# Fewer projections in step with the first modulation, and gates in two branches, in a two-layer diffusion block on one Trainium2 core

## The chip, the core and the metric

The kernel runs on one core of a Trainium2 chip. Time is the device time of one execution in microseconds (us); smaller is better. A profile is one further execution recorded by the hardware profiler. The engines are TensorE (PE, with its weight loads PEld), VectorE (DVE), ScalarE (ACT), GpSimd (POOL) and SyncE (SP), whose queue issues nearly all transfers.

## The reference, cut to what matters

Two layers work on 256 context and 256 latent tokens with width 2048, in float32. Each layer normalises, applies a shift and a scale that come from a conditioning vector (the modulation), runs a mixer, projects and adds. Layer 0 is a bidirectional gated DeltaNet:

```python
qkv, z, ba = jnp.split(h @ w_in, [DN_CONV_CH, DN_CONV_CH + DN_VW], axis=-1)
q, k, v = jnp.split(short_conv_silu(qkv, conv_w), [DN_QK, 2 * DN_QK], axis=-1)
beta = jax.nn.sigmoid(ba[:, :, :, 0])
g = -jnp.exp(a_log) * jax.nn.softplus(ba[:, :, :, 1] + dt_bias)
...
gc = jnp.cumsum(chunks(g), axis=-1)
decay = jnp.where(incl, jnp.exp(jnp.where(incl, diff, 0.0)), 0.0)
lower = jnp.where(strict, jnp.einsum('nbhid,nbhjd->nbhij', kb, kc) * decay, 0.0)
tinv = triangular_solve(eye + lower, eye)
```

There are 16 key heads ("groups" in the kernel), each with two value heads and two directions, and chunks of tokens that are solved with an inverse and then joined by a recurrence. Layer 1 is differential attention; the change doesn't touch it.

## The kernel before, in words

Tokens lie along the free axis (512 of them), the width along partitions in 16 k-tiles. A float32 projection is done as three matmuls on split operands (hi x hi, hi x lo, lo x hi), 16 k-tiles x 3 matmuls of 512 columns each.

The program has these stages. First the early stage, lines 260 to 325. The modulation of layer 0 is computed by `ada_pair`, 16 pairs of 256 outputs, each from four tiles `ar` of 512 KB (`ada_load`, 12 buffers); each pair ends in a copy (`arow`), small matmuls and `ada_put`. Pair 0 stands ahead of the loads of x (`xt`), which feed the sum of squares (`acc0`) and the row of reciprocal roots (`rrow0`, line 284). Then eight steps follow; each computes two pairs, makes two k-tiles of h (`make_h`: multiply by `rrow0` on GpSimd, scale and shift on ScalarE, split into `hhi` and `hlo`) and runs these two k-tiles of the six projections in the list `EARLY`: ba (the inputs of beta and decay), k0, q0, v00, v01 and k1, in PSUM tiles so, pj, pj, iv, iv and sb. The activated conditioning row `rc` is written to DRAM as `sc_d` from ScalarE's queue (line 324); the later modulations read it back through tiles `cr`.

Then `gates` (lines 375 to 461) turns ba into the tables `gct`, `lnb`, `eg`, `egl`, `kd`: a copy, four transposes, a softplus on both halves at once (line 415 to 427: 512 columns), the product with `ea` (line 434), cumulative sums by matmul, and the same sums as rows through four staging copies `gt_gr` to DRAM as `gc_d` (line 447). `adt` and `convw` are loaded just before, on SP's queue.

After it, generators write the instructions in an order that a planner (`Drive`) sets by priorities and estimated costs. `filler` writes the projections in a fixed order (k0, q0, v0, v1 of group 0, k1, then for each group z0, z1, next q, v0, v1, and k two ahead); those in `early` are only finished. `post_k`, `post_q`, `post_v`, `post_z` do convolution and activation. `stream_m` builds the masked matrices m of a group: `decay` loads rows of `gc_d` into `grm`, subtracts `gct`, takes the exponential; `block_inv` sends them through DRAM (`mb_d`), inverts 16 x 16 blocks on VectorE and stores them in `tu_d`. `stream_lev` joins the blocks in three levels to `uf`. `stream_at` does the same decays (`gra`) for the attention part. `stream_b` runs the recurrence, four steps a group, and needs v, uf and, in each half, at. Two streams compute the other modulations on GpSimd and ScalarE (`aw`, `rp`). A scheduler then fixes the order on each engine from the order written, priorities and a timing model; `tc.high_priority()` puts what it holds ahead.

Last come the two halves of the output projection (from about 2012 us) and layer 1.

Of the kernel before, what the change touches and what calls it, by code (L numbers as in the profile page):

```python
# [20 lines left out]
P = 128  # L21
T = 512
# [39 lines left out]
def body(ctx, tc, D, d, out):  # L62
# [197 lines left out]
    t0_cm = pool("t0")  # L260
# [10 lines left out]
    with tc.high_priority():  # L271
        ada_pair(0, 0, ada_load(0, 0, t0, "ar", 12), gq(), t0)
        xt = [hpool.tile([P, T], F32, tag="hlo", name=f"xt{kt}", bufs=KT) for kt in range(KT)]
        for kt in range(KT):
            nc.sync.dma_start(xt[kt], d["xT"][:, kt])
    with tc.high_priority():
        acc0 = t0.tile([P, T], F32, name="acc0")
        nc.scalar.activation(acc0, xt[0], AF.Square)
        for kt in range(1, KT):
            sq = t0.tile([P, T], F32, tag="mh", name=f"sq{kt}", bufs=2)  # L280
            nc.scalar.activation(sq, xt[kt], AF.Square)
            nc.vector.tensor_tensor(acc0, acc0, sq, ALU.add)
        rrow0 = t0.tile([P, T], F32, name="rrow0")
        nc.scalar.copy(rrow0, rstd_rows(acc0, T, lambda: so().rearrange("p a b i -> p (a b i)"),
                                         t0.tile([P, 4, P], F32, name="rr_dg0")))

    SK = 2
# [7 lines left out]
    np_ = 0  # L295
    for k0 in range(0, KT, SK):
        with tc.high_priority():
            for kind in range(2):
                if k0 + kind:
                    pr = kind * HKT + k0 // 2  # L300
                    ada_pair(0, pr, ada_load(0, pr, t0, "ar", 12), (gq, tr)[np_ % 2](), t0)
                np_ += 1
            for kt in range(k0, k0 + 2):
                make_h((xt[kt][:, 0:256], xt[kt][:, 256:512]), kt, rrow0, 0, hhi, hl, t0, nc.gpsimd)
        for n, src, _ in EARLY:
            w = SK * P
            r = t0.tile([P, w], F32, tag="er", name=f"e{n}r{k0}", bufs=4)
            nc.sync.dma_start(r, src[:, k0 * P:k0 * P + w])
            hi = t0.tile([P, w], F32R, tag="eh", name=f"e{n}h{k0}", bufs=8)
            lo = t0.tile([P, w], F32R, tag="el", name=f"e{n}l{k0}", bufs=8)  # L310
            split(hi, lo, r)
            for k in range(SK):
                kt, ks = k0 + k, slice(k * P, (k + 1) * P)
                ps = early[n]
                mm(ps, hi[:, ks], hhi[:, kt, :], kt == 0, False)
                mm(ps, hi[:, ks], hl(kt), False, False)
                mm(ps, lo[:, ks], hhi[:, kt, :], False, kt == KT - 1)
    rc = t0.tile([2, D], F32, name="rc")
    nc.sync.dma_start(rc, d["crow"])
    rth = t0.tile([2, D], F32, name="rth")  # L320
    nc.scalar.activation(rth, rc, AF.Tanh, scale=0.5)
    nc.vector.scalar_tensor_tensor(rc, rth, 1.0, rc, ALU.add, ALU.mult)
    nc.vector.tensor_scalar(rc, rc, 0.5, None, ALU.mult)
    nc.scalar.dma_start(sc_d, rc)
# [35 lines left out]
    for i in range(2):  # L360
        for j in range(2):
            nc.sync.dma_start(full(tu_d[i][j]), zt.rearrange("p (u i) -> p u i", u=8))
# [128 lines left out]
    def ev(*k):  # L491
        return evs.setdefault(k, Event())
# [802 lines left out]
```

## Time and profile before

| | |
|---|---|
| median of 3 runs | 3181.67 us (3176.39 to 3182.67) |
| the profiled execution | 3170.24 us, its span 3168.5 us |
| busy share of the span | PE 89%, PEld 71%, DVE 62%, ACT 59%, POOL 64% |
| moved by DMA | 457.06 MB, mean 144 GB/s |
| mean granted clock of TensorE | 0.954 of 2.4 GHz |

A share is a mean over stages with different limits, so the stretches of the next section but one count for more than this table. A granted clock of 0.50 is 1.2 GHz.

### The profile page before, as it was taken

The page shows a single profiled execution, that of the slowest core. Times are in us where ns is not written, and L with a number is a line of the kernel's source. Part 1 is how long each engine was busy: PE and PEld are TensorE (multiplying, and loading weights), DVE is VectorE, ACT ScalarE, POOL GpSimd, SP SyncE. Part 2 cuts the span into 40 slices and gives each one's busy share as a digit, 9 for nine tenths or more (in the row PEclk, how much of TensorE's full clock was granted, in tenths as well). Part 3 has the DMA queues.
Part 4 walks back from the last instruction along what each step waited for, and adds up shares of the span by engine and source line. Part 5 has one row for each costly group of instructions (what it writes and reads, how often), then busy time and mean ns, then how long its engine had stood idle before and what let it go on. Part 6 is the DMA issues. An engine that isn't in the chain of part 4 may idle for free.

```text
span 3168.5 us, 52448 instructions
## 1 busy us (share of the span) xinstructions
PE 2833.0 (89%) x16178; PEld 2236.6 (71%) x16178; DVE 1980.1 (62%) x4274; ACT 1863.0 (59%) x5466; POOL 2026.2 (64%) x2370
## 2 busy tenths in 40 slices
PE   4977888888998988998988988899898999999998
PEld 1555666676776766776766766677686888888888
DVE  2148768778778688588688688632334664545454
ACT  3545666666766766766666666654455665434354
POOL 2567677777787777777777777566466677322234
PEclk6988999999999999999999999999999999999999
DMA  9645445455545555545455546656744454333345
GB/s 362 223 114 118 123 119 135 123 133 118 139 134 129 127 126 133 128 129 136 122 125 131 132 118 134 173 171 189 230 147 132 144 164 150 123 110 113 117 127 164
DMA packets 511795, 457.06 MB, mean 144 GB/s; under 512 B 241684, under 2 KB 383764, under 8 KB 511508
## 3 DMA queue, kind: packets, MB, share of 16 engines
q1 hardware_dynamic: 511508, 453.68, 51.8%
q8 instruction: 127, 2.08, 0.3%
q14 instruction: 156, 1.28, 0.1%
q10 hardware_dynamic: 4, 0.02, 0.0%
HBM read 427.18 MB, written 26.36 MB: 143 GB/s over the span
## 4 chain that ended last, share of the span: by engine, by line
PE 33%; DVE 26%; DMA 19%; ACT 7%; POOL 7%; issue 5%; SPq 2%; POOLq 0%; DVEq 0%; ACTq 0%
PE pj L83 28%; DMA gra<-gc_d 5%; POOL rp L138 4%; DMA grm<-gc_d 4%; DVE bP L712 4%; DVE grm L687 3%; DMA aw<-in_adaw_dram 3%; DVE gra L687 2%; DVE bY L714 2%; ACT rp L139 2%; DVE R L783 1%; PE sb L83 1%; DMA ar<-in_adaw_dram 1%; PE iv L83 1%; DVE ma L695 1%
## 5 line engine op out<-in xcount | busy, mean ns | idle before, releaser
L139 ACT ACTIVATE rp<-rp 128x256 f32<-128x256 f32 x1024 | 426.9, 417 | 378.6 <-POOL rp L138 375.5
L712 DVE TENSOR_TENSOR bP<-bX,bY 64x1 f32<-64x1 f32 (+14 forms) x480 | 228.8, 477 | 18.1 <-ACT bY L710 9.8
L139 ACT ACTIVATION_READ_ACCUMULATOR rp<-rp 128x1 f32 x1024 | 194.0, 189 | 0.0
L687 DVE TENSOR_SCALAR gra<-gra,gct,lnb 128x128 f32<-128x128 f32 x256 | 114.3, 488 | 97.9 <-DMA gra<-gc_d 97.2
L687 DVE TENSOR_SCALAR grm<-grm,gct,lnb 128x128 f32<-128x128 f32 x256 | 144.9, 610 | 47.9 <-DMA grm<-gc_d 47.3
L783 DVE TENSOR_TENSOR R<-iv,lv 128x512 f16<-128x512 f32 x192 | 126.1, 678 | 32.8 <-PE iv L83 32.6
L689 ACT ACTIVATE grm<-grm 128x512 f32<-128x512 f32 x64 | 40.4, 631 | 132.0 <-DVE grm L687 127.1
L83 PEld LDWEIGHTS <-m 128*128 128x128 f16 x1024 | 74.2, 100 | 62.0 <-issue 57.7
L714 DVE TENSOR_REDUCE bY<-bP 64x1 f32<-64x1 f32 (+14 forms) x480 | 108.8, 227 | 8.7
L83 PE MATMUL iv<-U,R 128*128 128x128 f16 x768 | 75.7, 223 | 34.4 <-DVE R L783 30.0
L83 PEld LDWEIGHTS <-R 128*128 128x128 f16 x768 | 47.6, 99 | 77.6 <-DVE R L783 44.6
L745 POOL TENSOR_TENSOR ma<-ma,cs 128x512 f32<-128x512 f32 x64 | 85.3, 1333 | 20.7 <-DVE ma L695 18.3
L83 PE MATMUL sb<-yb,uf 128*128 128x128 bf16 x512 | 54.2, 225 | 40.7 <-ACT yb L879 22.2
L689 ACT ACTIVATE gra<-gra 128x512 f32<-128x512 f32 x64 | 40.4, 631 | 84.1 <-DVE gra L687 84.1
L83 PE MATMUL iv<-T,m 128*128 128x128 f16 x768 | 71.4, 223 | 15.8 <-ACT T L800 7.2
L224 DVE TENSOR_TENSOR hlo<-mh,hhi 128x512 fp32r<-128x512 f32 x32 | 29.6, 929 | 86.8 <-ACT hhi L223 77.8
L748 POOL TENSOR_TENSOR ml<-ma,m 128x512 bf16<-128x512 f32 x64 | 76.1, 1189 | 10.5 <-ACT m L747 10.3
L83 PEld LDWEIGHTS <-uf 128*128 128x128 f16 x512 | 36.4, 100 | 64.6 <-issue 59.1
L801 ACT CAST U<-iv 128x512 f16<-128x512 f32 x128 | 75.7, 591 | 0.0
L800 ACT CAST T<-iv 128x512 f16<-128x512 f32 x128 | 73.7, 576 | 3.0 <-PE iv L83 2.9
L83 PE MATMUL so<-x,at 128*128 128x128 f32 x512 | 71.6, 280 | 3.8 <-DVE x L911 2.7
L83 PEld LDWEIGHTS so<-x,at 128*128 128x128 f32 x512 | 64.9, 194 | 6.2 <-DVE x L911 3.6
(2758 smaller groups left out, 11429.3 us busy)
## 6 DMA issues: line engine op xcount, KB each, us to landing
aw<-in_adaw_dram SPq DMA_DIRECT2D x512, 128.0 KB, 3.0
ar<-in_adaw_dram SPq DMA_DIRECT2D x64, 512.0 KB, 7.3
gra<-gc_d SPq DMA_DIRECT2D x128, 128.0 KB, 4.2
grm<-gc_d SPq DMA_DIRECT2D x128, 128.0 KB, 4.1
mb_d<-m SPq DMA_DIRECT2D x32, 256.0 KB, 3.7
T<-tu_d SPq DMA_DIRECT2D x128, 64.0 KB, 2.7
U<-tu_d SPq DMA_DIRECT2D x128, 64.0 KB, 2.7
yd<-sz SPq DMA_DIRECT2D x32, 256.0 KB, 3.4
```

The lines of the kernel that those rows point to most:

```text
L83: nc.tensor.matmul(o, l, r, start=start, stop=stop)
L138: nc.gpsimd.tensor_tensor(pr, r, cr[:, s], ALU.mult)
L139: nc.scalar.activation(pr, pr, AF.Copy, accum_out=acc[:, s, q:q + 1])
L687: nc.vector.tensor_scalar(gr[:, u], gr[:, u], gct[:, c, dd, j:j + 1], lnb[:, c, dd, j:j + 1], ALU.subtract, ALU.min)
L689: nc.scalar.activation(gr, gr, AF.Exp)
L712: nc.vector.tensor_tensor(pr[:, :i, :i], X[:, i, :i].unsqueeze(1).to_broadcast([64, i, i]), Y[:, :i, :i].rearrange("p j c -> p c j"), ALU. ...
L714: nc.vector.tensor_reduce(Y[:, i, :i], pr[:, :i, :i], AX.X, ALU.add)
L745: nc.gpsimd.tensor_tensor(ma, ma, ident.unsqueeze(1).to_broadcast([P, 4, P]), ALU.add)
L748: nc.gpsimd.tensor_tensor(ml[:, :, k], mv, m16[:, :, k], ALU.subtract)
L783: nc.vector.tensor_tensor(R, quad(pp), lvb(n), ALU.mult)
L800: nc.scalar.copy(Tm, quad(pt))
L801: nc.scalar.copy(U, quad(pu))
```

## The change

- x is loaded ahead of everything in the early stage; pair 0 of the modulation goes into the first step.
- `EARLY` keeps only ba, k0 and q0; v00, v01 and k1 become ordinary jobs of `filler`. `iv` now serves the rstd row.
- The tiles of the early stage move to a pool `ta` with 8 `ar` buffers for 12, 6 `er`, `eh` and `el` for 4, 8 and 8; the projections are written inside `tc.high_priority()` too.
- `rc` is laid out over 128 partitions, computed at the very start, and stored to `sc_d` only in `gates`, after the exponential for `eg`.
- `convw` and `adt` are loaded at the end of the early stage, into a pool `gp` that also keeps the tables.
- `gates` takes the two softplus branches apart: decay (256 columns) first, then the row sums in two stores for four, then the beta branch.
- The zeroing of `tu_d` stands behind `gates`.
- `stream_lev` no longer waits for the convolutions of v0 and v1 of group 0; `stream_at` waits for `tu(0, 1)` in group 0.

```diff
+    W2 = 2 * D // P
+    rc = gp.tile([P, W2], F32, name="rc")
+    nc.sync.dma_start(rc, d["crow"].rearrange("s (p i) -> (s p) i", i=W2))
...
-    with tc.high_priority():
-        ada_pair(0, 0, ada_load(0, 0, t0, "ar", 12), gq(), t0)
...
-    EARLY = [("ba", d["wba"], so()), ("k0", d["win"][0, 1], pj()), ("q0", d["win"][0, 0], pj()),
-             ("v00", d["win"][0, 2], iv()), ("v01", d["win"][0, 3], iv())]
-    if G > 1:
-        EARLY.append(("k1", d["win"][1, 1], sb()))
+    EARLY = [("ba", d["wba"], so()), ("k0", d["win"][0, 1], pj()), ("q0", d["win"][0, 0], pj())]
...
+    with tc.high_priority():
+        for kt in range(KT):
+            nc.sync.dma_start(xt[kt], d["xT"][:, kt])
...
+        nc.scalar.copy(rrow0, rstd_rows(acc0, T, iv, ta.tile([P, 4, P], F32, name="rr_dg0")))
+        np_ = 0
+        for k0 in range(0, KT, SK):
             for kind in range(2):
-                if k0 + kind:
-                    pr = kind * HKT + k0 // 2
-                    ada_pair(0, pr, ada_load(0, pr, t0, "ar", 12), (gq, tr)[np_ % 2](), t0)
+                pr = kind * HKT + k0 // 2
+                ada_pair(0, pr, ada_load(0, pr, ta, "ar", 8), (gq, tr)[np_ % 2](), ta)
                 np_ += 1
...
-    nc.scalar.dma_start(sc_d, rc)
...
+        convw = load_small("convw", [P, 4 * KT, 5], d["convw"], gp)
+        adt = load_small("adt", [P, 2, 2, HV],
+                         d["adt"].to_broadcast([P, NB]).rearrange("p (k d h) -> p k d h", k=2, d=2), gp)
...
+        nc.vector.tensor_tensor(t2[1], ba[:, :, :, 1, :], wide(adt[:, 1]), ALU.add)
+        nc.vector.tensor_copy(bt, ba[:, :, :, 0, :])
...
+        def softplus(k):
+            t, e, u, w = t2[k], tl(f"e{k}", sh), tl(f"u{k}", sh), tl(f"w{k}", sh)
+            nc.scalar.activation(e, t, AF.Abs)
+            nc.scalar.activation(e, e, AF.Exp, scale=-1.0)
+            nc.vector.tensor_scalar(u, e, 2.0, None, ALU.add)
+            nc.vector.reciprocal(w, u)
...
+            return w
+
+        w = softplus(1)
+        g = tl("g", sh)
         nc.vector.tensor_tensor(g, w, wide(ea), ALU.mult)
...
+        for a in range(2):
+            p3 = (gq, tr)[a]()
+            for c in range(2):
+                for dd in range(2):
+                    q = 2 * c + dd
+                    mm(p3[:HV, q * P:(q + 1) * P], g[:, 2 * a + c, dd, :], tri(dd))
+            r = tl(f"r{a}", [HV, 4, P])
+            nc.scalar.copy(r.rearrange("p q i -> p (q i)"), p3[:HV])
+            nc.sync.dma_start(gc_d[2 * a:2 * a + 2].rearrange("c (d h) i -> h (c d) i", d=2), r)
...
+        nc.vector.tensor_scalar(lnb, softplus(0), -1.0, None, ALU.mult)
+        tc.keep_in_program_order(nc.scalar.activation(eg, p1v, AF.Exp))
+        tc.keep_in_program_order(nc.scalar.dma_start(sc_d.rearrange("s (p i) -> (s p) i", i=W2), rc))
...
+        nc.vector.tensor_tensor(gct, raw, lnb, ALU.subtract)
...
     def stream_lev(p):
-        yield ev("conv", 0, "v0")
-        yield ev("conv", 0, "v1")
...
             yield ev("kT", g)
             yield ev("qT", g)
+            if g == 0:
+                yield ev("tu", 0, 1)
```

## Rows read from the trace of the kernel before

**Rows 1.** Windows: busy us (x instructions) by engine, clock, DMA share, GB/s.
```profile
0.00:75.00 75.00, 33.35 (x250) 12.20 (x250) 17.41 (x29) 23.03 (x49) 12.53 (x17) 0.65 0.97 363
75.00:186.00 111.00, 105.03 (x628) 65.76 (x628) 14.47 (x18) 59.81 (x174) 73.30 (x100) 0.98 0.62 203
186.00:342.00 156.00, 107.81 (x475) 81.55 (x476) 125.40 (x234) 82.31 (x254) 106.99 (x121) 0.82 0.46 114
342.00:2012.00 1670.00, 1491.56 (x8798) 1151.14 (x8798) 1279.94 (x2957) 1104.59 (x3446) 1246.92 (x1549) 0.96 0.52 129
```

**Rows 2.** Windows, ten microseconds of the early stage, same columns.
```profile
30.00:40.00 10.00, 2.32 (x20) 0.40 (x16) 7.01 (x10) 6.48 (x12) 0.94 (x1) 0.50 1.03 392
```

**Rows 3.** Timeline of ScalarE: start, us, instruction, idle before it and releaser.
```profile
72.00 0.50 ACTq L324 DMA_DIRECT2D sc_d<-rc  x1
72.54 0.59 ACT L284 COPY rrow<-so 128x512 f32<-128x512 f32 x1 [16.20 <-DMA ar<-in_adaw_dram]
```

**Rows 4.** Timeline of TensorE: first and last projection matmuls of the early stage.
```profile
76.70 0.63 PE L83 MATMUL pj<-hhi,ek0h 128*128 128x512 f32 x1
77.13 0.63 PE L83 MATMUL pj<-hhi,eq0h 128*128 128x512 f32 x1
...
184.60 0.40 PE L83 MATMUL sb<-hhi,ek1l 128*128 128x512 f32 x1
184.83 0.60 PE L401 MATMUL gq<-cs,gt_baT 128*128 128x128 f32 x4
```

**Rows 5.** Timeline of ScalarE: first uf; recurrence begins in groups 1 and 15.
```profile
342.20 0.58 ACT L790 CAST uf<-iv 128x512 f16<-128x512 f32 x1
...
441.86 0.61 ACT L879 CAST yb<-v 128x512 bf16<-128x512 f32 x1
...
2030.51 0.61 ACT L879 CAST yb<-v 128x512 bf16<-128x512 f32 x1
```

**Rows 6.** DMA issues from 0 to 186 us: count, KB each, us to landing.
```profile
ar<-in_adaw_dram SPq DMA_DIRECT2D x64, 512.0 KB, 7.3
xt<-in_xT_dram SPq DMA_DIRECT2D x16, 256.0 KB, 6.0
...
ebar<-in_wba_dram SPq DMA_DIRECT2D x8, 128.0 KB, 4.1
```

**Rows 7.** Timeline of TensorE: modulation tiles at full and half clock, small matmuls.
```profile
12.11 0.64 PE L83 MATMUL tr<-ar,sc 128*32 128x256 f32 x8 [0.24 <-DMA ar<-in_adaw_dram]
...
17.89 0.61 PE L83 MATMUL tr<-sel,arow 128*128 128x2 f32 x4
...
62.66 1.08 PE L83 MATMUL gq<-ar,sc 128*32 128x256 f32 x8 [1.68 <-DMA ar<-in_adaw_dram]
```

**Rows 8.** Timeline of VectorE in the gates.
```profile
189.90 0.20 DVE L432 TENSOR_SCALAR gt_ea<-gt_ea 128x64 f32<-128x64 f32 x1 [11.19 <-ACT gt_ea L431]
...
195.76 3.35 DVE L420 RECIPROCAL gt_w<-gt_u 128x512 f32<-128x512 f32 x1
...
212.61 0.94 DVE L434 TENSOR_TENSOR gt_g<-gt_w,gt_ea 128x256 f32<-128x256 f32 x1
...
215.09 1.75 DVE L451 RECIPROCAL beta<-gt_e 128x256 f32<-128x256 f32 x1
...
236.12 1.00 DVE L459 TENSOR_TENSOR gct<-gct,lnb 128x256 f32<-128x256 f32 x1
...
243.38 0.67 DVE L582 COPY kT<-tr 128x512 f32<-128x512 f32 x1
```

**Rows 9.** Timelines of VectorE and SP in the first decays, and the page's DMA issues.
```profile
251.14 1.66 DVE L687 TENSOR_SCALAR gra<-gra,gct,lnb 128x128 f32<-128x128 f32 x4 [1.64 <-DMA gra<-gc_d]
...
267.79 0.38 SPq L701 DMA_DIRECT2D mb_d<-m  x1
...
grm<-gc_d SPq DMA_DIRECT2D x128, 128.0 KB, 4.1
```

**Rows 10.** Weight splits of group 2's k on ScalarE: ns min/median/max, first and last start.
```profile
L185 ACT CAST g2khi<-g2kr x8: 387/410/449, 310.8 to 329.7; 128x256 fp32r<-128x256 f32 x8
```

More of the change, by code (lines that the diff above doesn't have):

```diff
@@ L258, in so @@
         return psm.tile([P, 2, 2, P], F32, tag="so", name="so", bufs=1)
-    t0_cm = pool("t0")
+    gp_cm = pool("gp", side="right")
+    gp = gp_cm.__enter__()
+    gct, eg, kd, egl, lnb = (gp.tile([P, NCH, 2, HV], F32, name=n) for n in ("gct", "eg", "kd", "egl", "lnb"))
+    zt = gp.tile([P, P], F16, name="zt")
+    nc.vector.memset(zt, 0.0)
+    t0_cm = pool("t0", reuse_waits="tile")
     t0 = t0_cm.__enter__()
@@ L305, in body @@
[L305 to L323, printed above, removed]
-    nc.scalar.dma_start(sc_d, rc)
+                make_h((xt[kt][:, 0:256], xt[kt][:, 256:512]), kt, rrow0, 0, hhi, hl, ta, nc.gpsimd)
+            for n, src, _ in EARLY:
+                w = SK * P
+                r = ta.tile([P, w], F32, tag="er", name=f"e{n}r{k0}", bufs=6)
+                nc.sync.dma_start(r, src[:, k0 * P:k0 * P + w])
+                hi = ta.tile([P, w], F32R, tag="eh", name=f"e{n}h{k0}", bufs=6)
+                lo = ta.tile([P, w], F32R, tag="el", name=f"e{n}l{k0}", bufs=6)
+                split(hi, lo, r)
+                for k in range(SK):
+                    kt, ks = k0 + k, slice(k * P, (k + 1) * P)
+                    ps = early[n]
+                    mm(ps, hi[:, ks], hhi[:, kt, :], kt == 0, False)
+                    mm(ps, hi[:, ks], hl(kt), False, False)
+                    mm(ps, lo[:, ks], hhi[:, kt, :], False, kt == KT - 1)
@@ L355, in body @@
     dl = dl_cm.__enter__()
-    zt = dl.tile([P, 1024], F16, name="zt", tag="m16", bufs=4)
-    nc.vector.memset(zt, 0.0)
-    full = lambda a: a.rearrange("u (j i) -> j u i", i=P)[:P]
-    diag = lambda a: bass.AP(tensor=a[:].tensor, offset=a[:].offset, ap=[[16 * P + 16, 64], [P, 16], [1, 16]])
-    for i in range(2):
-        for j in range(2):
-            nc.sync.dma_start(full(tu_d[i][j]), zt.rearrange("p (u i) -> p u i", u=8))
-    convw = load_small("convw", [P, 4 * KT, 5], d["convw"], dl)
@@ L427, in gates @@
-        nc.vector.scalar_tensor_tensor(f5(w2), f5(t2), 0.0, f5(w2), ALU.max, ALU.add)
-        nc.vector.tensor_scalar(lnb, w2[:, 0], -1.0, None, ALU.mult)
-        e, t, w = e2[:, 0], t2[:, 0], w2[:, 1]
-        ea = t1.tile([P, 2, HV], F32, name="ea", tag="jk", bufs=1)
+        t2 = [tl(f"t{k}", sh) for k in range(2)]
+        bt = tl("bt", sh)
+        nc.vector.tensor_tensor(t2[1], ba[:, :, :, 1, :], wide(adt[:, 1]), ALU.add)
+        nc.vector.tensor_copy(bt, ba[:, :, :, 0, :])
+        ea = tl("ea", [P, 2, HV])
@@ L454, in gates @@
-        nc.scalar.activation(egl, p2[:, :n].rearrange("p (c d h) -> p c d h", c=NCH, d=2), AF.Exp)
-        nc.scalar.activation(eg, gct, AF.Exp)
-        nc.vector.tensor_tensor(fl(t), p2[:, :n], fl(gct), ALU.subtract)
+        t = tl("kt", sh)
+        nc.vector.tensor_tensor(fl(t), p1[:, n:2 * n], fl(raw), ALU.subtract)
         nc.scalar.activation(t, t, AF.Exp)
         nc.vector.tensor_tensor(kd, t, beta, ALU.mult)
-        nc.vector.tensor_tensor(gct, gct, lnb, ALU.subtract)
-    gates()
+    gates(early.get("ba"))
@@ L463, in conv_silu @@
+    full = lambda a: a.rearrange("u (j i) -> j u i", i=P)[:P]
+    diag = lambda a: bass.AP(tensor=a[:].tensor, offset=a[:].offset, ap=[[16 * P + 16, 64], [P, 16], [1, 16]])
+    for i in range(2):
+        for j in range(2):
+            nc.sync.dma_start(full(tu_d[i][j]), zt.unsqueeze(1).to_broadcast([P, 8, P]))
     def conv_silu(ps, ci, nm):
```

133 lines of the change are left out of this document (57 added, 76 removed).

## Prediction

> **What bounds the kernel now.** I read the busy time by stretch first, because one share for the whole span hides that the kernel has stages. The reader should see three things there [rows 1]. Up to 75 us the DMA engines are 97% busy and TensorE less than half: this stretch is bound by transfers. From 75 to 186 us it is the reverse: TensorE is busy 105.03 of 111 us, and the DMA engines 62%. From 186 to 342 us no unit is full in that way: TensorE has 48 us idle and VectorE, busy 125.40 of 156 us, is the most loaded. After that, in the main loop, TensorE is busy 1491.56 of 1670 us (89%).
>
> The timeline then shows what each boundary is. At 10 us a stretch the transfers run at 392 GB/s while TensorE works 2.32 of 10 us at half of its clock, 1.2 GHz [rows 2]. ScalarE holds the store of sc_d at the head of its queue until 72.00 us, and the rstd row that every h tile needs is copied only behind it, at 72.54, after 16.20 us of idling [rows 3]. So the six early projections begin at 76 us, and the last of their matmuls issues at 184.60; 0.23 us later the transposes of the gates begin, which tells that the gates wait for TensorE, and that TensorE carries k1, a projection the gates don't need, to the last [rows 4]. From there a chain of VectorE and DMA work runs to the first finished inverse factor, uf, at 342.20; the recurrence of group 1 starts at 441.86 and that of group 15 at 2030.51, so the main loop takes (2030.51 - 441.86)/14 = 113.5 us a group [rows 5]. I take the kernel as three pieces in series: early stage (to 184.8), first chain (157.4 us, to 342.2), and the rest, 2826 us, which the change touches only by what it hands over.
>
> **The early stage.** The change takes out three of six projections: 3 x 16 x 3 = 144 matmuls. They follow each other every 0.23 us at full clock and every 0.43 us at half clock [rows 4], so 33 us of TensorE leave the stretch that TensorE binds. What is left: 64 modulation tiles of 512 KB, 16 of x of 256 KB, 24 weight tiles of 128 KB [rows 6], together 40.9 MB. At 392 GB/s [rows 2] that is 104.3 us; at the 363 GB/s that the first 75 us kept up with their pauses [rows 1] it is 112.7 us. A step (two k-tiles; eight steps) moves 4.59 MB, 11.7 us at 392 GB/s. Its TensorE work at full clock is 8 x 0.64 + 2 x 0.61 + 18 x 0.23 = 10.5 us; at half clock 8 x 1.08 + 2 x 1.2 + 18 x 0.43 = 18.8 us [rows 4, 7]. So TensorE would be some 90% busy, and stretches as busy as that ran at 0.98 of full clock [rows 1]. I take transfers as the bound, with full clock. x first lets the rstd row come early, and the sc_d store no longer stands before it. The fewer modulation buffers (8 tiles for 12) are still one whole step of transfers ahead. Behind the last tile come its matmuls, the copy, the additions, one h tile (72.54 to 76.70 took 4.2 us [rows 3, 4]) and 18 matmuls: I put 11 us. The first issue is within 1 us. End of the stage: 112.7 + 1 + 11 = 125 us, 60 us earlier than now. Bounds: 104.3 + 1 + 11 = 116 us (69 earlier), and, at half clock throughout, 11.7 for x plus 8 x 18.8 = 162 us (23 earlier).
>
> **The gates.** adt is loaded inside the early stage. Now VectorE stands idle 11.19 us until 189.90, while the transposes were out at 185.4 [rows 4, 8]: 4.5 us less. Splitting the gates makes two sets of half the columns. A reciprocal takes 3.35 us on 512 columns and 1.75 on 256 [rows 8], so the stretch from 194.8 us to the product with ea at 212.61 (17 us without lnb) makes 9 us a branch. Decay branch first: about 3 us of reads and ScalarE, 9, the product with ea 0.94, and the convolution of k0 in between (3 us): 16 us. The second branch adds about 10.5 and the subtraction 1.0: the decay table gct is complete some 28 us after the start. Now it is complete at 237.1, 47 us after 190.0 [rows 8], because four staging copies, one PSUM tile and one staging tile are passed in turn between. That is 19 us. Writing the rows to DRAM (two stores for four) runs under the second branch. Against this, the k tile that the first decay also needs is copied at 243.38 [rows 8], and its own chain shares VectorE with the gates; so of 4.5 + 19 I count 18 us. Bounds: 0 (the k tile as late after the stage as now) and 23.5.
>
> **The order of the decays.** The attention decays of group 0 now wait for tu(0, 1). Today three gra decays stand before or between the first grm decays; VectorE waits for them at 251 us, and the first masked tile goes to DRAM at 267.79 [rows 9], 23.7 us after the k tile. Without them: the first decay is loaded before the k tile is there, the second needs its load (4.1 us), its VectorE, ScalarE and GpSimd passes, in all some 12 us. I take 11 us saved; bounds 0 (another wait in the same queue) and 12. The gra decays come due later, beside the 36 us of inverse steps, which is their cover; without it they cost those 11 us back. That the inverse steps no longer wait for v0 and v1 changes nothing in the sum: those tiles are early.
>
> **What moves.** The 33 us of TensorE go into the first chain, as the first jobs of the filler; v0, v1, k1 stand before z, q and v of the next groups there. TensorE has 48 us idle in it at clock 0.82 [rows 1]. A chain shorter by 29 us leaves 19; a fuller engine at higher clock gives back up to 15 (107.81 x (0.95 - 0.82)/0.95). That is 34, just enough on paper, but the main loop, too, leaves 11% unused, 14 us of 128. So some 16 us of projections are late when the recurrence starts; I charge 12. Bounds 0 and 33. The late modulation loads that ran from 96 us under the early stage also start later, because sc_d is written after the gates; GpSimd and ScalarE have room for them in the main loop and behind it (by stretch 75% and 66% busy [rows 1]), so I charge nothing. If that room were not there, a part of the 73.30 us that GpSimd worked from 75 to 186 us would come due a second time [rows 1]. The sc_d store on ScalarE's queue now stands behind the exponential of the gates; the exponential for egl and the convolutions of q0 and v0 queue behind it, and what it held up before was 16.20 us [rows 3], in a stretch of full transfers; after the stage they are 46% busy [rows 1]. Zeroing of tu_d moves behind the gates on SP's queue; it is needed some 100 us later.
>
> The Trainium skill bears on the last term. Perfetto Trace Analysis, section Optimization Strategy, says that a kernel whose most contended engine changes over time may gain by interleaving the regimes; this change takes TensorE work out of a transfer-bound stage, so by that page all 33 us would be paid and the sum would be 56 us. The trace agrees only in part: 75 to 186 us is bound by TensorE already [rows 1].
>
> **Sum.** 60 + 18 + 11 - 12 = 77 us off the profiled 3170.24: 3093. The median of the runs, 3181.67, is 11.4 us above that execution, so 3105. All best ends: 69 + 23.5 + 12 = 105, 3077. All worst: 23 + 0 + 0 - 33, a 10 us loss.
>
> **Rivals.** (1) Half clock: with fewer projections TensorE waits for each step's tiles, as from 0 to 75 us where the mean clock was 0.65 [rows 1], and never rises; the stage ends at 162, the sum is 23 + 29 - 12 = 40, time 3142. Against it: at 18.8 us a step TensorE would be full, and full stretches ran at 0.98. The Trainium skill, TensorE: Matmul & The Clock Gate, section HAM oscillation, describes this: a loop whose matmuls are short against its wait for DMA falls to the low clock at every step. The first 75 us agree with it (0.65), the stretch behind them, at 0.98, doesn't show it [rows 1]. Chance of this rival: 0.15. (2) The moved matmuls are paid in full, since main-loop idling is made of waits in a fixed order that other work can't fill: 60 + 29 - 33 = 56, time 3126. Chance 0.17. (3) Slower: the filler, three projections behind, never catches up; k and v of the next group arrive late for its decays, and every group takes longer than 113.5 us. From 77/14 = 5.5 us a group on it outweighs the gain; 7 us makes 98, time 3203. For it: TensorE is the busiest engine of the loop. Against it: the weights of group 2's k were split by 330 us, 112 us before the recurrence of group 1 began [rows 5, 10]. Chance 0.08. (4) It doesn't do what it says: the main loop sets its own end whatever it starts with, since TensorE has the same work in all; time 3182 within 6 us. Against it: TensorE lost 42 us to idling before 75 us and 48 us in the first chain [rows 1]. Chance 0.05. My forecast has 0.55, own range 3085 to 3125.
>
> **Numbers.** 3105. The range from 3075 to 3165 takes in rivals 1 and 2 and the bounds but the two worst together, and leaves out (3), (4) and a little at the low end, under 0.2. A measurement tells about 0.2%, 6.4 us, from no change. Faster 0.86 (forecast, 1, 2, less 0.01), same 0.06, slower 0.08.
>
> **What would show it.** Transposes of the gates near 125 us with the clock near 1.0 from about 40 us on; the rstd row before 30; no wait for adt; gct complete some 28 us after; the first grm decay before any gra; first uf near 253; 113 to 115 us a group. Wrong if the transposes come after 145, if uf is not at least 60 us earlier, or if the group period rises by 3 us or more.

## The result, and the profile after

The changed kernel took 3140.32 us (median of 4 runs, 3137.56 to 3143.46) beside 3179.03 us for the kernel before (4 runs, 3172.59 to 3182.67): a ratio of 0.9884 [0.9869, 0.9900], some 39 us. The forecast had 77. The sign was right, the size half; 3140 lies inside the range and outside the forecast's own one. The profiled execution took 3137.95 us (span 3136.1), 32 us less than that of before, whose median lay further above its profile.

The busy time by stretch of the changed kernel, cut where its stages end (start and end of the stretch, its length, then the engines, granted clock, DMA share, GB/s):

```profile
core 0: us, PE busy (x) PEld busy (x) DVE busy (x) ACT busy (x) POOL busy (x), PEclk, DMA share, GB/s
0.00:75.00 75.00, 40.58 (x278) 19.75 (x278) 15.33 (x34) 31.00 (x70) 20.84 (x32) 0.84 0.98 340
75.00:130.00 55.00, 47.80 (x376) 29.20 (x376) 5.18 (x8) 23.26 (x61) 21.12 (x28) 0.84 0.95 347
130.00:149.00 19.00, 14.85 (x80) 10.51 (x80) 3.40 (x7) 6.55 (x17) 3.18 (x4) 0.82 0.04 16
149.00:294.00 145.00, 117.91 (x537) 89.21 (x536) 116.75 (x246) 73.25 (x210) 94.08 (x110) 0.92 0.48 114
294.00:1982.00 1688.00, 1506.98 (x8849) 1165.11 (x8849) 1275.72 (x2948) 1110.07 (x3451) 1239.05 (x1554) 0.96 0.52 127
```

Transfers now bind to the end of the early stage: a DMA share of 0.95 until 130 us at 347 GB/s, where before [rows 1] TensorE was full. In the early stage TensorE idles 46 us in 149, beside 48 in 186 before: the stage is shorter by about what was taken out of it. What was won in TensorE's idle time was won in the first chain: 27 us in 145 beside 48 in 156 [rows 1].

The timelines of the changed kernel at the milestones (start, us, engine, line, instruction, idle before it and what ended that; `bT` is the first copy of a finished block inverse):

```profile
17.08 4.53 SPq L169 DMA_DIRECT2D ar<-in_adaw_dram  x8
21.97 9.73 SPq L466 DMA_DIRECT2D tu_d<-zt  x4
27.58 0.58 ACT L304 COPY rrow<-iv 128x512 f32<-128x512 f32 x1 [9.19 <-PE iv L83]
31.75 1.03 SPq L316 DMA_DIRECT2D ebar<-in_wba_dram  x1
...
136.05 1.50 PE L83 MATMUL tr<-ar,sc 128*32 128x256 f32 x24
138.10 0.61 PE L83 MATMUL tr<-sel,arow 128*128 128x2 f32 x4 [0.55 <-ACT arow L178]
141.86 0.79 PE L83 MATMUL so<-hhi,ebah 128*128 128x512 f32 x1 [3.15 <-ACT hhi L223]
142.45 0.63 PE L83 MATMUL pj<-hhi,ek0h 128*128 128x512 f32 x1
142.87 0.63 PE L83 MATMUL pj<-hhi,eq0h 128*128 128x512 f32 x1
...
148.54 0.66 PE L395 MATMUL gq<-cs,gt_baT 128*128 128x128 f32 x4
179.15 0.43 DVE L449 TENSOR_TENSOR gct<-gt_x,lnb 128x256 f32<-128x256 f32 x1
195.79 0.69 DVE L587 COPY kT<-tr 128x512 f32<-128x512 f32 x1
211.35 0.37 SPq L706 DMA_DIRECT2D mb_d<-m  x1
239.80 0.40 ACT L722 CAST bT<-bY 32x256 f16<-32x256 f32 x1 [1.35 <-DVE bY L719]
293.91 0.57 ACT L793 CAST uf<-iv 128x512 f16<-128x512 f32 x1
388.46 0.61 ACT L884 CAST yb<-v 128x512 bf16<-128x512 f32 x1
2000.33 0.62 ACT L884 CAST yb<-v 128x512 bf16<-128x512 f32 x1 [0.32 <-PE sb L83]
```

The rstd row is there at 27.58 instead of 72.54 [rows 3], but SP issues the first modulation tile only at 17.08, and behind the first eight the zeroing of tu_d holds its queue for 9.7 us, at a place where the forecast did not have it: the scheduler moved it up, since it waits for nothing. The gates' transposes come at 148.54 (before 184.83 [rows 4]; forecast 125). The decay table is complete 31 us after them (forecast 28, before 52). The k tile, though, follows 47.3 us after the transposes (before 58.5 [rows 4, 8]), the first masked tile 15.6 us after the k tile (before 24.4 [rows 8, 9]), and the first uf at 293.91 instead of 342.20 [rows 5], 48 us earlier where 89 were forecast. The recurrence of group 1 leads by 53 us, that of group 15 by 30: (2000.33 - 388.46)/14 = 115.1 us a group, 1.6 more than before [rows 5].

### The profile page after: what moved, and what is told of

It reads as the page before. It is cut to its first block, busy times and chain, and to the rows that moved or that the text cites. A ratio compares the mean times of both kernels' runs of the same rounds, so it can differ in the third digit from the quotient of the medians.

```text
span 3136.1 us, 52478 instructions
## 1 busy us (share of the span) xinstructions
PE 2826.4 (90%) x16178; PEld 2242.2 (71%) x16178; DVE 1965.8 (63%) x4287; ACT 1861.2 (59%) x5466; POOL 2009.7 (64%) x2370
## 4 chain that ended last, share of the span: by engine, by line
PE 30%; DVE 10%; DMA 7%; POOL 3%; ACT 3%; issue 2%; SPq 0%; DVEq 0%; POOLq 0%; ACTq 0%
PE pj L83 26%; DMA gra<-gc_d 2%; POOL rp L138 2%; DVE bP L717 1%; DMA grm<-gc_d 1%; PE at L83 1%; DVE grm L692 1%; DVE gra L692 1%; DMA aw<-in_adaw_dram 1%; PE sb L83 1%; ACT rp L139 1%; DVE bY L719 1%; PE iv L83 0%; PE so L83 0%; DMA yr<-yd 0%
## 5 line engine op out<-in xcount | busy, mean ns | idle before, releaser
L717 DVE TENSOR_TENSOR bP<-bX,bY 64x1 f32<-64x1 f32 (+14 forms) x480 | 220.0, 458 | 16.7 <-ACT bY L715 9.0
```

The lines of the kernel that those rows point to most:

```text
L717: nc.vector.tensor_tensor(pr[:, :i, :i], X[:, i, :i].unsqueeze(1).to_broadcast([64, i, i]), Y[:, :i, :i].rearrange("p j c -> p c j"), ALU. ...
```

## Theories

A: TensorE's ordered projections pace the main loop, and the end moves with them, not with the first chain. B: the first uf starts everything and the end follows it. C, formed on the first four runs, when neither was enough: both must be there, in the changed kernel they are about level, and the end follows the later one. P, a rival to all three: an edit also moves the order of the main loop's instructions, and this order is worth tens of us by itself.

All kernels that were run, with the first uf and the rest of the span behind it in the profiled execution (before: 342.20 and 2826.3; changed kernel: 293.91 and 2842.2):

| kernel | edit against the changed kernel, if not said otherwise | us, median | ratio to before | first uf | rest |
|---|---|---|---|---|---|
| e_zero_late | tu_d zeroed after the early stage | 3128.80 | 0.9846 [0.9831, 0.9860] | 284.65 | 2841.4 |
| z_ar | that, and one modulation pair ahead of x | 3134.72 | 0.9853 [0.9828, 0.9878] | 287.95 | 2844.8 |
| e_at_first | attention decays don't wait | 3153.25 | 0.9920 [0.9901, 0.9939] | 307.00 | 2845.6 |
| e_beta_first | beta branch first | 3148.92 | 0.9905 [0.9888, 0.9923] | 299.23 | 2846.1 |
| e_six | six projections early | 3162.27 | 0.9954 [0.9938, 0.9971] | 313.56 | 2845.6 |
| b_three | kernel before, three early | 3175.17 | 0.9985 [0.9972, 0.9997] | 321.78 | 2850.8 |
| z_two | zeroing late, two early | 3141.36 | 0.9885 [0.9858, 0.9912] | 279.85 | 2860.0 |
| z_five | zeroing late, five early | 3158.13 | 0.9925 [0.9903, 0.9948] | 300.76 | 2858.0 |
| e_no_inv0 | no inverse steps in group 0 | 3141.54 | 0.9881 [0.9861, 0.9900] | 247.96 | 2883.1 |
| e_less_pe | 128 matmuls left out | 3124.98 | 0.9832 [0.9813, 0.9852] | 297.27 | 2828.3 |
| e_six_no_inv0 | both of their edits | 3138.75 | 0.9875 [0.9858, 0.9892] | 266.93 | 2868.5 |
| e_less_pe_no_inv0 | both of their edits | 3116.79 | 0.9796 [0.9767, 0.9825] | 249.50 | 2866.1 |
| z_f70 | zeroing late, planner's price 0.70 | 3167.08 | 0.9949 [0.9931, 0.9967] | 277.43 | 2892.6 |
| z_f62 | zeroing late, planner's price 0.62 | 3131.13 | 0.9854 [0.9834, 0.9873] | 290.72 | 2838.7 |
| z_lat36 | zeroing late, planner's due time 36 | 3138.37 | 0.9869 [0.9844, 0.9894] | 285.30 | 2842.4 |
| z_five_f70 | z_five, planner's price 0.70 | 3172.40 | 0.9982 [0.9969, 0.9994] | 301.54 | 2871.6 |
| b_f70 | kernel before, planner's price 0.70 | 3205.20 | 1.0084 [1.0067, 1.0102] | 348.06 | 2852.5 |
| b_f62 | kernel before, planner's price 0.62 | 3157.22 | 0.9929 [0.9907, 0.9952] | 345.45 | 2814.7 |

## Experiments on the early stage

**e_zero_late** takes the tile of zeros from the later pool again, as the kernel before did; the stores then wait for the early stage to end.

```diff
-    zt = gp.tile([P, P], F16, name="zt")
-    nc.vector.memset(zt, 0.0)
...
+    zt = dl.tile([P, 1024], F16, name="zt", tag="m16", bufs=4)
+    nc.vector.memset(zt, 0.0)
-            nc.sync.dma_start(full(tu_d[i][j]), zt.unsqueeze(1).to_broadcast([P, 8, P]))
+            nc.sync.dma_start(full(tu_d[i][j]), zt.rearrange("p (u i) -> p u i", u=8))
```

> The changed kernel, with the tile of zeros taken from the later pool, as before the change, so that the four zeroing transfers of tu_d follow the last modulation tile on SP's queue. In the changed kernel they sit at 22 to 32 us, ahead of the second step's tiles. Both theories: the early stage ends 8 to 10 us before 148.5, everything behind it moves along, the end 3130 to 3133 us. If the transfers had been hidden: stage end and time unchanged, 3137 to 3143.

Measured 3128.80 us, and the two intervals don't touch: the early zeroing costs 11.5 us. Its timelines:

```profile
139.95 2.56 SPq L466 DMA_DIRECT2D tu_d<-zt  x4
132.78 0.79 PE L83 MATMUL so<-hhi,ebah 128*128 128x512 f32 x1 [3.15 <-ACT hhi L223]
139.44 0.66 PE L393 MATMUL gq<-cs,gt_baT 128*128 128x128 f32 x4
284.65 0.59 ACT L793 CAST uf<-iv 128x512 f16<-128x512 f32 x1 [0.48 <-PE iv L83]
```

Four stores that held SP for 9.73 us among the loads take it 2.56 us here; their source differs too (one row of zeros spread over eight before, a whole tile here), so the runs don't tell how much of this is the place. The transposes come 9.1 us earlier, the first uf 9.3, the end 10.1 in the profiled executions. The wait for the last h tile and the half clock behind it are the same as in the changed kernel.

**z_ar** loads the first modulation pair ahead of x, as the kernel before did, on top of e_zero_late.

```diff
+        ar0 = list(ada_load(0, 0, ta, "ar", 8))
         for kt in range(KT):
             nc.sync.dma_start(xt[kt], d["xT"][:, kt])
...
-                ada_pair(0, pr, ada_load(0, pr, ta, "ar", 8), (gq, tr)[np_ % 2](), ta)
+                ada_pair(0, pr, ada_load(0, pr, ta, "ar", 8) if pr else ar0, (gq, tr)[np_ % 2](), ta)
```

> The same as z_two's base (three early, zeroing late) with the first modulation pair's four loads ahead of x, as before the change, so that x comes after 2 MB more. The row of factors comes some 5 us later, the first modulation's matmuls some 8 to 15 us sooner. If the early stage is bound by its bytes (45 MB by 139 us), the order of its first 10 MB doesn't matter: transposes at 137 to 142, end 3125 to 3132. If x first is worth what it brings forward: transposes some 5 us later, end 3132 to 3136.

The rstd row comes 2.5 us later (31.54), the transposes 3.4 us later (142.81), the first uf 3.3. The interval overlaps that of e_zero_late, so in time no difference is shown: what x first is worth by itself, 3.3 us by the first uf, isn't clear of noise.

## Experiments on the first chain

**e_at_first** takes back the wait of group 0's attention decays.

```diff
-            if g == 0:
-                yield ev("tu", 0, 1)
```

> The changed kernel without the wait of the second decays of group 0 for the inverses, so that they are made at once when the keys and queries of group 0 are there, as in the kernel before. The step of the forecast that this undoes was priced at 11 us by the row of the second decay ahead of the first ones: the first inverse should start some 9 to 11 us later. Theory C: the inverse steps after it are then free of those decays, so that the first uf moves by -4 to +4 us only, and the end by as little: 3136 to 3146. The forecast's step as written: uf 11 us later and the end 3151.

Its timelines, with one of the four loads of attention decays that VectorE waits for:

```profile
198.57 0.69 DVE L587 COPY kT<-tr 128x512 f32<-128x512 f32 x1
207.44 0.84 DVE L692 TENSOR_SCALAR gra<-gra,gct,lnb 128x128 f32<-128x128 f32 x2 [3.10 <-DMA gra<-gc_d]
214.93 1.01 DVE L692 TENSOR_SCALAR gra<-gra,gct,lnb 128x128 f32<-128x128 f32 x2 [1.31 <-DMA gra<-gc_d]
228.03 0.38 SPq L706 DMA_DIRECT2D mb_d<-m  x1
307.00 0.57 ACT L793 CAST uf<-iv 128x512 f16<-128x512 f32 x1
```

The attention decays stand between the k tile and the first masked tile again; that tile goes out 29.5 us after the k tile instead of 15.6, the first uf comes 13 us later and the end 12.9. The forecast's 11 us were about right, and they arrive at the end. My expectation, that the first uf would move by 4 us at most, was wrong.

**e_beta_first** makes the beta branch's softplus ahead of the decay branch's.

```diff
+        nc.vector.tensor_scalar(t2[0], bt, -1.0, None, ALU.mult)
+        wb = softplus(0)
         w = softplus(1)
...
-        nc.vector.tensor_scalar(t2[0], bt, -1.0, None, ALU.mult)
-        nc.vector.tensor_scalar(lnb, softplus(0), -1.0, None, ALU.mult)
+        nc.vector.tensor_scalar(lnb, wb, -1.0, None, ALU.mult)
```

> The changed kernel with the beta branch's softplus (some 16 instructions on VectorE, two on ScalarE) made before the decay branch instead of after it, so that the cumulative sums wait for both, as they did before the change. Theory C: the cumulative decays, and with them the first inverse and the first uf, come 7 to 10 us later, the projections don't move, and a chain that comes later than level costs what it comes later: 3145 to 3150. Theory A (projections alone): 3138 to 3143, no change.

3148.92 us, 8.6 more, as C forecast, but with an interval that still overlaps the changed kernel's; the k tile comes 9.2 us later (205.01), the first uf 5.3, less than the 7 to 10 expected.

## Experiments on the list of early projections

**e_six** runs v00, v01 and k1 early again, in the changed kernel.

```diff
-    EARLY = [("ba", d["wba"], so()), ("k0", d["win"][0, 1], pj()), ("q0", d["win"][0, 0], pj())]
+    EARLY = [("ba", d["wba"], so()), ("k0", d["win"][0, 1], pj()), ("q0", d["win"][0, 0], pj()),
+             ("v00", d["win"][0, 2], iv()), ("v01", d["win"][0, 3], iv()), ("k1", d["win"][1, 1], sb())]
...
-        nc.scalar.copy(rrow0, rstd_rows(acc0, T, iv, ta.tile([P, 4, P], F32, name="rr_dg0")))
+        nc.scalar.copy(rrow0, rstd_rows(acc0, T, tr, ta.tile([P, 4, P], F32, name="rr_dg0")))
```

> The changed kernel, with v00, v01 and k1 back among the early projections (rstd row through another PSUM tile); all other parts of the change kept. Theory A (TensorE's ordered projections pace the main loop, so the end moves with the filler's lead, not with the first uf): the early stage ends 10 to 25 us later than 148.5, because TensorE's 46 idle us in it take up part of the 33, but the filler's z0 of group 0 begins at 165 to 185 us where it began at 201.6, and the end comes 10 to 25 us earlier: 3115 to 3130 us. Theory B (the first uf sets the end; the 23 us lost in the loop have another cause): uf comes 10 to 20 us later than 293.9 and the end with it: 3150 to 3160 us.

Its timelines:

```profile
170.71 0.60 PE L396 MATMUL gq<-cs,gt_baT 128*128 128x128 f32 x4
313.56 0.59 ACT L794 CAST uf<-iv 128x512 f16<-128x512 f32 x1
2026.93 0.63 ACT L885 CAST yb<-v 128x512 bf16<-128x512 f32 x1
```

3162.27, a little above B's 3150 to 3160: the short list is worth 22 us here: transposes 22.2 us later, first uf 19.7, end 23.1 in the profiled executions. A has no place for this, since 34 us of TensorE's work were done sooner.

**b_three** is the opposite: the kernel before with the short list alone (the inverse levels don't wait for v0 and v1, as in the change).

```diff
-    EARLY = [("ba", d["wba"], so()), ("k0", d["win"][0, 1], pj()), ("q0", d["win"][0, 0], pj()),
-             ("v00", d["win"][0, 2], iv()), ("v01", d["win"][0, 3], iv())]
-    if G > 1:
-        EARLY.append(("k1", d["win"][1, 1], sb()))
+    EARLY = [("ba", d["wba"], so()), ("k0", d["win"][0, 1], pj()), ("q0", d["win"][0, 0], pj())]
...
-        yield ev("conv", 0, "v0")
-        yield ev("conv", 0, "v1")
```

> The kernel before with the shorter list alone: beta/decay, k0 and q0 run early, v00, v01 and k1 are left to the main loop's filler, and the inverse levels don't wait for the v convolutions; nothing else of the change. The counterpart, everything but the short list, gave 3162, 16 us less than before. Theory C (the end follows the later of TensorE's projections and the chain of group 0): 34 us of matmuls leave an early stage that TensorE filled after 75 us, so its transposes come at 151 to 158 instead of 184.8, the first uf about 28 us sooner, and the end by the rest of the change's 38 us: 3156, range 3148 to 3164. A rival (the short list is worth nothing where the first rows of x come late): 3172 to 3182.

0.15% faster, where C had 3148 to 3164 and its rival 3172 to 3182: the edit that names the change is worth some 5 us alone, the rest alone (e_six) 15, both together 39. Its timelines show that it did what it should, and lost it:

```profile
73.02 0.59 ACT L284 COPY rrow<-so 128x512 f32<-128x512 f32 x1 [16.61 <-DMA ar<-in_adaw_dram]
158.29 0.66 PE L398 MATMUL gq<-cs,gt_baT 128*128 128x128 f32 x4
321.78 1.06 ACT L785 CAST uf<-iv 128x512 f16<-128x512 f32 x2
2038.11 0.62 ACT L874 CAST yb<-v 128x512 bf16<-128x512 f32 x1
```

Transposes 26.5 us earlier and first uf 20.4, but the recurrence of group 15 begins 7.6 us later than before.

**z_two** and **z_five** run two and five early, with the zeroing late (in z_five the rstd row goes through another PSUM tile, as in e_six).

```diff
-("k0", d["win"][0, 1], pj()), ("q0", d["win"][0, 0], pj())]
+("k0", d["win"][0, 1], pj())]                                        # z_two
+("k0", d["win"][0, 1], pj()), ("q0", d["win"][0, 0], pj()),          # z_five
+             ("v00", d["win"][0, 2], iv()), ("v01", d["win"][0, 3], iv())]
```

> The changed kernel with the zeroing back behind the early stage (3128.8 alone) and only beta/decay and k0 early; q0 too goes to the filler. TensorE is idle for 45 us of the early stage, so 11 us of q0's matmuls taken out of it should hardly shorten it (its transposes at 135 to 139 instead of 139.4), while the queries of group 0 come later. Theory C: 3125 to 3135, no gain left in a shorter list. The rival that each projection fewer is worth what the three were (22 / 3 = 7 us): 3118 to 3124.

> The same with five early: beta/decay, k0, q0, v00 and v01. 23 us of TensorE's work go back into the early stage, of which idle time takes a part: transposes at 148 to 158 instead of 139.4, first uf 9 to 15 us later. Theory C (a chain that comes late costs what it comes late): 3138 to 3146. The rival (TensorE's total work and idle alone, moved work costs nothing): 3126 to 3131.

Two early took 3141.36 (transposes 141.94, not earlier than with three), five 3158.13 (transposes 159.44); both lie above all that was expected of them. Three is best at this order; but five lost 29 us with a first uf only 16 us later, so 13 us of it came after the first uf, where C has nothing that could cost them. With two, the first uf came 4.8 us earlier than in e_zero_late and the end 12.6 us later.

## Experiments on what sets the end

**e_no_inv0** leaves out the fifteen inverse steps of group 0 (those inverses stay the identity); **e_less_pe** leaves out two of three matmuls of z0 and z1 in groups 1 and 2, 30 us of TensorE; the other two kernels have the first edit each on top of e_six and of e_less_pe.

```diff
-        for i in range(1, 16):
+        for i in range(1, 16 if g else 1):
...
-                        mm(ps, hi[:, ks], hh(kt), kt == 0, False)
-                        mm(ps, hi[:, ks], hl(kt), False, False)
-                        mm(ps, lo[:, ks], hh(kt), False, kt == KT - 1)
+                        if kind in ("z0", "z1") and g in (1, 2):
+                            mm(ps, lo[:, ks], hh(kt), kt == 0, kt == KT - 1)
+                        else:
...
```

> The changed kernel, leaving out the 15 steps of the block inverse in group 0 (both halves, 60 VectorE instructions, some 20 us of the first chain; the inverse of group 0 is then not computed). Theory A: the first uf comes about 20 us earlier, the end moves by at most 8 us: 3132 to 3145. Theory B: the end moves with uf, 15 to 25 us: 3115 to 3125.

> The changed kernel, leaving out two of the three matmuls of each k-tile of z0 and z1 in groups 1 and 2 (128 matmuls, 30 us of TensorE at 0.234 us; the gate path of these groups loses precision). Their weights are still loaded and split. Theory A: the end comes 20 to 30 us earlier: 3110 to 3120. Theory B: the main loop has room in TensorE, the end moves by at most 8 us: 3132 to 3143.

> The changed kernel with v00, v01 and k1 back among the early projections, and with the fifteen inverse steps of group 0 left out (those inverses stay the identity), so both edits of two earlier runs at once. Theory C (two things end together in the changed kernel, TensorE's ordered projections and the chain of group 0, and the end follows the later one): with six early projections the chain was 20 us late and the projections 12 us ahead (34 us of work done early, stage 22 us longer); with the inverse left out as well the chain is about 26 us ahead, so the projections set the end: 3140 - 12 = 3128, range 3120 to 3136. Rival N (the 3162 of the six came from an order of the main loop that the planner happened to draw, not from the late chain): it stays at 3150 to 3165.

> The changed kernel with two of three matmuls of z0 and z1 left out in groups 1 and 2 (128 matmuls, 30 us of TensorE) and the fifteen inverse steps of group 0 left out. Alone the one gave 15 us and the other nothing. Theory C (the end follows the later of projections and chain, about level in the changed kernel): with both moved the sum shows, 3140 - 30 = 3110, range 3103 to 3117. Theory A (TensorE's projections alone pace the end, and half of the matmuls left out were hidden for another reason): 3125, as without the second edit, range 3119 to 3131.

The first uf and the recurrences of groups 1 and 15 in e_no_inv0:

```profile
247.96 1.07 ACT L793 CAST uf<-iv 128x512 f16<-128x512 f32 x2
355.93 0.60 ACT L884 CAST yb<-v 128x512 bf16<-128x512 f32 x1
1994.53 0.62 ACT L884 CAST yb<-v 128x512 bf16<-128x512 f32 x1
```

A first uf 46 us earlier moved the end by nothing (3141.54): its lead in the recurrence fell from 33 us in group 1 to 6 in group 15. That speaks against B: only an order worse by about 46 us could hide such a gain, more than the 38 us that the order alone is seen to cost below. Leaving out 30 us of matmuls gave 15, which is half of A. On e_six, the same missing inverse gave 23.5 us, where C forecast 34; on e_less_pe it gave 8, where C forecast 15. C, formed on the first two of these runs, has the right sign in the other two, with sizes a third and a half short; the 8 us are not clear of noise, since the two intervals overlap.

## Experiments on the order of the main loop

Here no instruction is added, removed or resized. The planner prices three matmuls of a projection at 0.65 us and makes an inverse due 32 us after it is begun; these numbers decide only in which order the streams are written out, and the traces have the same number of instructions on each engine.

```diff
-                        yield 0.65, 0.0
+                        yield 0.70, 0.0        # z_f70, z_five_f70, b_f70; 0.62 in z_f62 and b_f62
...
-                dr.set("tu", g, half, lat=32)
+                dr.set("tu", g, half, lat=36)   # z_lat36
```

> The changed kernel with the zeroing late (3128.8), and in the planner's list the price of a projection's three matmuls 0.70 us instead of 0.65: no instruction added, removed or resized, only the order in which the main loop's streams are written out. Theory C: the first uf stays at 285 +-5 and the end with it, 3124 to 3134. Rival P (the order drawn is worth tens of us by itself, so that differences of 10 to 30 us between kernels with other orders need no other cause): outside 3118 to 3140.

> The three-early, zeroing-late kernel with the planner's due time for a group's inverse 36 instead of 32 us: order only. Theory C: 3124 to 3134. Rival P: outside 3118 to 3140.

> Five early projections, zeroing late (3158.1), with the same repricing from 0.65 to 0.70 us. Theory C with five early: the first uf stays near 301 and the end at first uf + 2844 = 3145 to 3160. Rival P: the 29 us that the two v projections cost were mostly the order, and this comes below 3140.

> The kernel before (3179) with the planner's price of three matmuls 0.70 instead of 0.65 us: order only. From its first uf at 342 to its end the kernel before took 2826 us, the changed one 2842. If that 16 us is what moved matmuls cost (the forecast's term, 12), a new order leaves the kernel before within 6 us of itself: 3173 to 3185. If the kernel before merely had a good order, it comes out slower: 3186 to 3200.

> The three-early, zeroing-late kernel (3128.8) with the planner's price of a projection's three matmuls 0.62 instead of 0.65 us: order only. At 0.70 it took 3167, the kernel before 3205. If the price has one direction (dearer projections are written out sparser, and the last groups' chain falls behind them), a lower price gives the same or less: 3115 to 3130. If the order is a draw, it may be anywhere from 3120 to 3165.

> The kernel before (3179) with that price at 0.62 instead of 0.65 us: order only. At the same price the change with the zeroing late was worth 50 us at 0.65 and 38 us at 0.70. If the change's worth is its own and not its order's, 30 to 55 us lie between this and z_f62, wherever the two come out.

The order alone can be worth tens of us, as P says: a price of 0.70 costs the best kernel 38 us (C had it within 5) and the kernel before 26 (3205, above even the 3186 to 3200 that the loss of a good order was to give); 0.62 leaves the best kernel where it was and gives the kernel before 22. z_f70 had the earliest first uf of all kernels that leave nothing out (277.43). The copy of group 10's keys, first in z_f70 and then in e_zero_late:

```profile
1333.90 0.69 DVE L587 COPY kT<-tr 128x512 f32<-128x512 f32 x1
```

```profile
1274.95 0.68 DVE L587 COPY kT<-tr 128x512 f32<-128x512 f32 x1
```

From group 7 on, the keys of z_f70 are copied 37 to 85 us later than there, although its last weights are split at about the same time (ScalarE's last split of group 15's z1 begins at 1970.5, beside 1964.0). I read this as keys that wait for their place in the order and not for their weights; no run tests that reading by itself.

The traces show how far the order moves. Take the matmuls that TensorE runs from 400 to 2000 us of one kernel (some 8300), name each by its tiles and its count, and compare their places in another kernel. A price of 0.70 moves a matmul by 78 places on average (z_f70 beside e_zero_late) and by 91 (b_f70 beside the kernel before), 0.62 by 21 and 16, a due time of 36 by 10. Edits that leave the planner's prices and waits alone move it too, beside the changed kernel by 42 in e_zero_late and 30 in e_no_inv0. But not every edit does: z_ar runs the changed kernel's main loop in exactly the same order, on all engines. In this one pair with a common order the first uf comes 6.0 us earlier, and the median 5.6 and the profiled end 3.4 us earlier, with intervals that overlap.

Not all of it fits P. z_lat36 took 3138.37, above C's 3134 and inside the 3118 to 3140 that P had left to C, with an interval that overlaps e_zero_late's. z_five_f70 was to come below 3140 by P and to 3160 at most by C, and took 3172.40; at 0.70 five early are thus 5 us behind three, at 0.65 they were 29. And one rival is left: the price may have a direction instead of giving a new draw each time. 0.70 is the slowest in both kernels, and the kernel before gets slower with every step of the price (3157, 3180, 3205). z_f62, at 3131.13, lies 1 us above the 3115 to 3130 of that rival and inside the range of a draw, which does not decide it.

At equal price the change with the zeroing late is worth 3157.22 - 3131.13 = 26 us (0.62), 3177.58 - 3128.80 = 49 us (0.65) and 3205.20 - 3167.08 = 38 us (0.70), each pair from runs on one chip. The 26 us lie below the 30 to 55 expected of b_f62, so the change's worth is not free of the order either. As written, with the zeroing early, it should be 11 us less; that was not run at the other two prices.

## Why the forecast was half right

Two steps of the forecast failed: the early stage, sized at 60 us and measured at 36.3, and the levels behind the inverse, put at nothing without a reason, where 11.7 us were lost. Of the 45 us missing, these are 23.7 and 11.7. The profiled executions, piece by piece: 36.3 (stage) + 11.3 (gates to k tile) + 8.8 (first masked tile) + 3.5 (inverse steps) - 11.7 (levels) - 15.9 (rest) = 32.3 us.

**The early stage: 60 forecast, 36.3 measured; the mechanism right, the size not.** Transfers bound it, as said, at 340 to 347 GB/s beside the 363 assumed. But they ended at 130 us and not at 113.7. I counted 40.9 MB; 44.86 MB were moved: constants, 1.25 MB of v's weights loaded ahead, 0.25 MB of a later modulation, and 1 MB of zeros, which cost 9.1 us of the stage (e_zero_late). "Zeroing of tu_d moves behind the gates on SP's queue" is the sentence that was wrong: I read the program order, and the scheduler moved up a store that had lost its dependence on the stage by having its source in another pool. Behind the last transfers I put 11 us, and 18.5 passed: TensorE idles 3.15 us for the last h tile and runs the next 12 of 18 matmuls at half clock (0.43 us apart; granted clock 0.50 from 141.8 to 146.7 us). Rival 1 gave 3142, nearly the measured time, but by another way and so by luck: the stage ended at 148.5 and not at 162, at a mean clock of 0.84.

**The gates and the k tile: 18 forecast, 11.3 measured.** The gates did what was said (31 us for 28). The bound 0 was there because the k tile might stay as late; it came 11 us earlier after the stage, and then it, not the decay table, was last. e_beta_first agrees with the gain of the leading branch (first uf 5.3 us later without it), though its time is not clear of noise.

**The order of the decays: 11 forecast, 13 in e_at_first; right.** Beside the kernel before, the first masked tile left 8.8 us sooner after the k tile.

**Not in the sum: the levels behind the inverse.** From the first copy of the inverse (bT) to the first uf took 42.4 us before, 54.1 after, and 45 to 55 in every other one with a whole inverse and the short list or the rest of the change; in the kernel before it stays 43 at all three prices. So of 29 us forecast for the chain 12 were got. One place can be shown, first in the kernel before and then in the changed one:

```profile
299.76 0.41 ACT L717 CAST bT<-bY 32x256 f16<-32x256 f32 x1 [4.19 <-DVE bY L714]
315.93 0.60 ACT L801 CAST U<-iv 128x512 f16<-128x512 f32 x1
319.57 0.40 PE L83 MATMUL iv<-T,m 128*128 128x128 f16 x4
```

```profile
255.39 0.58 ACT L804 CAST U<-iv 128x512 f16<-128x512 f32 x1
257.18 0.40 PE L83 MATMUL pj<-hlo,g1v0hi 128*128 128x512 f32 x1
259.82 1.22 PE L83 MATMUL gq<-kT 128*128 128x128 f32 x4 [2.25 <-DVE gm L699]
...
264.70 0.62 PE L83 MATMUL iv<-T,m 128*128 128x128 f16 x8
```

The T and U tiles of the first level are cast by 256 us. TensorE, in its order, stops after the first v matmuls: group 1's key products wait until VectorE's gm, here a step of group 0's attention decays, has read the PSUM tile gq that they write. It takes up the next level's matmuls only at 264.70. From the start of U's cast to those matmuls 9 us pass; before, 4. The levels now share TensorE's queue with the projections that were moved there, and with the attention decays, but which of these lengthens them by how much the runs don't tell apart: e_at_first (those decays ahead of the inverse) has 52, e_six (without those projections) 50.

**The moved projections: 12 charged, 16 paid** (rest 2826.3 before, 2842.2 after). The number was near, but its reason is not shown. With the projections taken back (e_six) the rest is not 12 to 16 us shorter than the changed kernel's 2842.2 but 2845.6; moved in the kernel before (b_three), they make it 24 us longer. The kernel before spans 2814.7 to 2852.5 us at three prices. A term of 12 us could not be forecast, or tested by one pair of kernels, under such a spread. That an edit can move the main loop's order, and that the order can be worth 38 us, was no part of my forecast; its range was wide enough by luck. The later modulations, charged nothing, cost nothing that shows: from the recurrence of group 15 to the end it is 1135.8 us beside 1138.0 before.

**The signs named beforehand:** the rstd row before 30, no wait for adt, the decay table some 28 us after (31) and the first masked decay ahead of any attention decay held; transposes at 125, clock 1.0 from 40 us and uf at 253 did not, and 115.1 us a group lies just above the 113 to 115. The text had called itself wrong if the transposes came after 145 or the uf not 60 us earlier: both happened.

What stays open: how much of the 39 us is the change and how much its order. At equal price 26 to 49 us were seen with the zeroing late, so the change gains at all three orders. Where a pair differs in the order of the main loop, a difference under some 25 us can be the order's. The edits to the early stage and the first chain behave better than that: in the changed kernel, e_zero_late, z_ar, e_at_first, e_beta_first and e_six the first uf moves over 29 us (284.65 to 313.56), and the rest stays within 5 us (2841.4 to 2846.1).

## What to carry to other kernels

Where a planner or scheduler writes the order of a long loop, run each edit at two or three settings that change nothing but that order, before a gain or loss is put down to the edit. A store that loses its dependence on a stage may rise into it: look where it is issued, not where it is written. In a stage bound by transfers count every byte that the scheduler can bring forward into it, and the half-clocked tail after the last wait.

The fastest kernel run with nothing left out is the changed one with the zeroing late: 3128.80 us, 0.9846 [0.9831, 0.9860] of before.

## What the hardware showed that was not expected

Four stores of 256 KB to DRAM, of zeros, in rows of 256 bytes took SP 9.73 us to issue and 8.0 us (median) to land among the loads, and 2.56 us to issue after them, there from another source tile. In the last step of the early stage TensorE ran at 1.2 GHz (granted clock 0.50) for some 5 us after its wait of 3.15 us for the h tile: the matmuls at 135.5 us were 0.23 us apart, those from 142.45 to 146.7 some 0.43, those from 147.1 on 0.23 again; e_zero_late has the same. That the order of a loop which no engine fills beyond 90% can be worth 22 to 38 us of 3150, with the same instructions, was the largest surprise.
